# Depthwise convolution by quarters of the channels, in steps between the half blocks of the gated product

## The chip, the cores and the metric

The kernel runs on one core of one Trainium2 chip. The metric is the device time of one execution in microseconds (us), as the median of several runs. Its engines are TensorE (PE, matmuls, with its weight loads PEld), VectorE (DVE), ScalarE (ACT), GpSimd (POOL) and SyncE (SP, whose queue issues the loads of the weights). They work side by side and wait for each other by semaphores. PSUM is the memory that matmuls write to, cut into buffers that are used in turn.

## The reference

A backbone of two layers over 256 context and 256 latent tokens (512 in all, D = 1024): layer 0 mixes tokens with a Conformer convolution, layer 1 with a bidirectional mLSTM, and each is followed by an MLP. The change lies in the convolution of layer 0:

```python
def conformer_conv(u, rows, w_pw1, b_pw1, w_dw, b_dw, ln_g, ln_b, w_pw2, b_pw2):
    a = u @ w_pw1 + b_pw1
    a = a[..., :CONV_DIM] * jax.nn.sigmoid(a[..., CONV_DIM:])
    ...
    a = jax.nn.silu(layer_norm(a + b_dw, ln_g, ln_b))
    return a @ w_pw2 + b_pw2
```

Where the dots are, `a` goes through a depthwise convolution with 31 taps, in rows of 64 tokens for the latent stream and over all 256 for the context. `u` is the input scaled and shifted by the adaLN map (`silu(c) @ ada_w`, 1024 x 6144 per layer), whose later columns give the gates and shifts of the layer's other steps. All is fp32.

## The kernel before, in words

**Products.** A large product takes its weights in column blocks of 128. A tile `raw` of 1 MB (two blocks) is loaded through SP's queue into one of three buffers; each block is split into a rounded part `wh` (ACT, L153) and a rest `wl` (DVE, L154, 128x1024), and every product of 128x128 by 128x512 is three matmuls: `wh` by the input's high part (L176), by its low part (L179), and `wl` by the high part (L180). A block of the gated product (`pw1`) is 8 x 3 = 24 of them.

**The start.** In the start loop, the adaLN map of the first two parts is made and the input split, and four blocks of `pw1` are accumulated beside it. They end with `pw1_epi`: for the gate half a sigmoid on ACT (L740), for the other a product on DVE (L744), which goes back to token order by four transposes (L747) into `A`. Then `gemm` (L215, steps at L218) runs the other 12 blocks, with `pw1_next` behind each.

**The convolution.** It is done as a Fourier transform of 128 points over the tokens. For each of four token tiles, `spectral(h, tt)` takes 512 channels at a time: a forward transform on PE (L762 for the context's tiles 0 and 1, with windows over neighbouring tiles; L767 for the latent tiles 2 and 3, two matmuls over 64 rows each), a multiplication by the spectrum's cosine and sine parts `Hc`, `Hs` on DVE (L776, L777), the inverse transform (L787, four matmuls into two column halves), the bias (L794) and the statistics (L795). It is called from `pw1_epi` for four tiles in a row, once when half of the channels are there and once at the end (`f % 4 == 3`). With the second half, `token_norm(tt)` (L799 on) joins the statistics, takes 1/sqrt by four Newton steps on a column of 128 values (`rsqrt`, L549 on), and applies the norm on DVE (L806).

**Tables.** The transforms' cosines come from a polynomial on DVE over 128x384 and 128x256 elements (L654 to L671), written before the gated product; the windows `ge32`, `lt32`, `ge96` are made on POOL, the spectrum by four matmuls over 31 rows (L693).

**Order.** A scheduler places each instruction on its engine's queue by its own estimate, in the order of the code where that does not decide; `keep_in_program_order` pins an instruction, `tc.issue_after(x)` puts what is inside behind x. Within `gemm`, two units of the adaLN map (`ada_g1`, L317) stand behind the blocks of `Z.fd`. Behind `gemm` come the loads of `pw2`, four units `ada_s2`, the activation `silu(0)` (transposes L845, ACT L848 and L849, DVE L850, the split at L153 and L154), and the product `pw2` with `ko=4`: its first four blocks are accumulated side by side, feature tile by feature tile, as the activation comes. The fifth block begins at 195.53 us of the trace.

## Time and profile before

| what | value |
|---|---|
| runs | 1729.02, 1731.77, 1736.95 us; median 1731.77 |
| the profiled execution | 1730.22 us, of which the span of its instructions 1728.5 us |
| mean granted clock of TensorE | 0.994 |
| gated product and first half of the convolution | 47.0 to 149.5 us of the span |
| second half, norms, activation, first four blocks of `pw2` | 149.5 to 195.5 us |

A page of the profile shows one execution on the slowest core. Busy times are by engine; in the view of windows each row is a stretch, with the busy us and the number of instructions of each engine, then PEclk (the granted clock of TensorE as a share of full speed), the share of DMA engines that were busy, and GB/s. A row of the timeline is start, duration, engine, line, operation, output and inputs, shape and count; in brackets the idle time of the engine ahead of it, and who ended it. Durations of neighbouring matmuls overlap, since they are pipelined: what one costs is the distance to the next start. An fp32 matmul has two records there, an fp32r matmul one.

### The profile page before, as it was taken

How to read it: one execution, taken by the hardware profiler on the slowest of the kernel's cores; microseconds unless marked ns; L12 is line 12 of the kernel's file. 1: busy time of each engine (PE TensorE's matmuls, PEld its weight loads, DVE VectorE, ACT ScalarE, POOL GpSimd, SP SyncE). 2: the span in 40 equal slices, each digit the busy share in tenths (PEclk: the TensorE clock that was granted, in tenths of full speed). 3: DMA queues.
4: the chain of work that ended last, by engine and by line, in shares of the span. 5: the costliest groups of instructions: out<-in, count | busy, mean ns of one | idle time of the engine just before them, and what ended most of it. 6: DMA issues, size and time to landing. Idle time of an engine off the chain costs nothing.

```text
span 1728.5 us, 23701 instructions
## 1 busy us (share of the span) xinstructions
PE 1688.9 (98%) x9270; PEld 1387.1 (80%) x9270; DVE 1064.0 (62%) x1918; ACT 743.1 (43%) x1193; POOL 61.3 (4%) x98
## 2 busy tenths in 40 slices
PE   8999999999999999999999999999999999989997
PEld 5655898878888999986688899888877878758886
DVE  5456895666645776772243663564487786777667
ACT  4311663231324465542232532442467564534453
POOL 0000000000000000000000000000011130030001
PEclk9999999999999999999999999999999999999999
DMA  9323524444423055568675753454445555656552
GB/s 361 144 106 129 191 74 171 152 140 147 146 98 146 26 177 168 161 215 280 239 222 178 248 173 116 153 187 167 169 173 190 194 192 191 243 212 213 184 186 95
DMA packets 69535, 300.58 MB, mean 174 GB/s; under 512 B 7026, under 2 KB 21874, under 8 KB 38704
## 3 DMA queue, kind: packets, MB, share of 16 engines
q1 hardware_dynamic: 51760, 284.39, 47.1%
q10 hardware_dynamic: 17664, 14.69, 2.6%
q8 instruction: 73, 1.20, 0.3%
q14 instruction: 38, 0.31, 0.1%
HBM read 283.32 MB, written 15.73 MB: 173 GB/s over the span
## 4 chain that ended last, share of the span: by engine, by line
PE 92%; DVE 4%; ACT 2%; DMA 1%; issue 1%; POOL 0%; SPq 0%; DVEq 0%; ACTq 0%; POOLq 0%
PE mm L176 17%; PE mm L180 17%; PE mm L179 17%; PE mm L189 7%; PE mm L190 3%; PE mm L206 3%; PE mm L207 3%; PE mm L205 3%; PE cv L207 2%; PE cv L205 2%; PE cv L206 2%; PE fl L317 2%; PE fl L718 1%; PE cv L787 1%; DVE wl L154 1%; PE ln L176 1%
## 5 line engine op out<-in xcount | busy, mean ns | idle before, releaser
L154 DVE TENSOR_TENSOR wl<-raw,wh 128x1024 fp32r<-128x1024 f32 x348 | 427.5, 1232 | 283.9 <-ACT wh L153 281.9
L153 ACT CAST wh<-raw 128x1024 fp32r<-128x1024 f32 x348 | 362.7, 1050 | 533.4 <-PE mm L179 319.8
L179 PE MATMUL mm<-u,wh 128*128 128x256 f32 (+1 forms) x960 | 322.7, 337 | 0.0
L176 PE MATMUL mm<-u,wh 128*128 128x256 f32 (+1 forms) x832 | 273.2, 330 | 6.1 <-DVE E L1003 2.5
L180 PE MATMUL mm<-u,wl 128*128 128x256 f32 (+1 forms) x832 | 272.2, 328 | 0.0
L179 PEld LDWEIGHTS mm<-u,wh 128*128 128x128 f32 x960 | 183.5, 191 | 18.2 <-DVE mv L553 0.8
L176 PEld LDWEIGHTS mm<-u,wh 128*128 128x128 f32 x832 | 159.2, 192 | 26.9 <-ACT wh L153 6.5
L180 PEld LDWEIGHTS mm<-u,wl 128*128 128x128 f32 x832 | 159.6, 192 | 16.0 <-DVE wl L154 1.7
L176 PE MATMUL mm<-xm,wh 128*128 128x512 f32 x256 | 102.9, 402 | 0.0
L205 PE MATMUL mm<-wh,xl 128*128 128x512 f32 x256 | 101.2, 396 | 0.0
L206 PE MATMUL mm<-wh,xl 128*128 128x512 f32 x256 | 100.9, 394 | 0.0
L180 PE MATMUL mm<-xm,wl 128*128 128x512 f32 x256 | 100.3, 392 | 0.0
L207 PE MATMUL mm<-wl,xl 128*128 128x512 f32 x256 | 99.6, 392 | 0.1
L176 PE MATMUL mm<-hid,wh 128*128 128x512 f32 (+1 forms) x256 | 93.3, 365 | 0.0
L179 PE MATMUL mm<-hid,wh 128*128 128x512 f32 (+1 forms) x256 | 92.8, 363 | 0.0
L180 PE MATMUL mm<-hid,wl 128*128 128x512 f32 (+1 forms) x256 | 92.8, 363 | 0.0
L189 PE MATMUL mm<-x,wh 128*128 128x512 f32 x248 | 86.8, 399 | 4.8 <-DVE x L1548 4.3
L393 DVE SCALAR_TENSOR_TENSOR S<-ar,cs,S 128x512 f32<-128x512 f32 x56 | 40.8, 750 | 60.5 <-DMA ar<-ada_w 60.4
L179 PE MATMUL mm<-qq,wh 128*128 128x272 f32 x256 | 73.9, 289 | 0.0
L176 PE MATMUL mm<-qq,wh 128*128 128x272 f32 x256 | 73.5, 288 | 0.0
L180 PE MATMUL mm<-qq,wl 128*128 128x272 f32 x256 | 73.5, 288 | 0.0
L189 PE MATMUL mm<-u,wh 128*128 128x512 f32 x192 | 68.7, 399 | 0.0
(482 smaller groups left out, 3296.5 us busy)
## 6 DMA issues: line engine op xcount, KB each, us to landing
raw<-w SPq DMA_DIRECT2D x64, 1024.0 KB, 4.9
raw<-wo SPq DMA_DIRECT2D x32, 1024.0 KB, 4.9
raw<-ada_w SPq DMA_DIRECT2D x28, 1024.0 KB, 4.9
ar<-ada_w SPq DMA_DIRECT2D x80, 256.0 KB, 3.4
raw<-wv SPq DMA_DIRECT2D x16, 1024.0 KB, 6.2
raw<-wqT SPq DMA_DIRECT2D x16, 1024.0 KB, 5.2
raw<-wq SPq DMA_DIRECT2D x16, 1024.0 KB, 4.9
raw<-wk SPq DMA_DIRECT2D x16, 1024.0 KB, 4.9
```

What stands on the lines that cost most here:

```text
L153: c = nc.scalar.copy(hi, src)
L154: nc.vector.tensor_tensor(lo, src, hi.bitcast(F32), op=ALU.subtract)
L176: a = nc.tensor.matmul(ps, wh, xh, start=start, stop=False)
L179: nc.tensor.matmul(ps, wh, xl, start=False, stop=False)
L180: nc.tensor.matmul(ps, wl, xh, start=False, stop=stop)
L189: todo = [lambda s_, e_: nc.tensor.matmul(ps, wh, r[0], start=s_, stop=e_), lambda s_, e_: nc.tensor.matmul(ps[:, :n], wl, r[0][:, :n], st ...
L190: lambda s_, e_: nc.tensor.matmul(ps[:, :n], wl, r[0][:, :n], start=s_, stop=e_)]
L205: nc.tensor.matmul(ps, xh, wh, start=start, stop=False)
L206: nc.tensor.matmul(ps, xl, wh, start=False, stop=False)
L207: nc.tensor.matmul(ps, xh, wl, start=False, stop=stop)
L317: a = nc.tensor.matmul(ps[32 * j:32 * j + 32], cs[:, kt, 14 - 2 * v:46 - 2 * v], blocks[kt], start=first and kt < 4, stop=last and kt >= 4 ...
L393: nc.vector.scalar_tensor_tensor(a, w, c, a, op0=ALU.mult, op1=ALU.add)
```

## The change

- The convolution goes by four quarters of 256 channels instead of two halves of 512. `spectral` is a generator: its first step is the forward transform with one multiplication on DVE by both parts of the spectrum (`HS`), its second the inverse with bias and statistics.
- Three of the quarters are side jobs of the gated product, at the middle and the end of each of its 12 blocks as `Z.jobs` says; each job does the forward part of one tile and the inverse of the tile before. The last quarter stays behind the product.
- The tables, windows and spectrum are side jobs too, the tables pinned, with the part that the spectrum needs first.
- One `ada_s2` unit moves into the loop (`Z.s2`), the `ada_g1` units move two blocks earlier (`Z.fd`); the load of the gate weights becomes the last side job.
- `token_norm(s)` does two tiles at once, on columns of two values, with three Newton steps of three operations; half of its application goes to ACT. DVE's work on tiles 2 and 3, and its splits of `pw2`'s weights, are put behind the norm of tiles 0 and 1.

```diff
 class Z:
-    fd = [3, 6, 7]
+    fd = [1, 4, 5]
+    s2 = [8]
+    jobs = [1, 1, 0, 1, 0, 1, 1, 1, 1, 1, 1, 1, 1, 1, 1, 1, 0, 1, 1, 1, 1, 1, 0, 0]
...
     def split(hi, lo, src):
         c = nc.scalar.copy(hi, src)
-        nc.vector.tensor_tensor(lo, src, hi.bitcast(F32), op=ALU.subtract)
+        with tc.issue_after(behind[0]) if behind else nullcontext():
+            nc.vector.tensor_tensor(lo, src, hi.bitcast(F32), op=ALU.subtract)
...
-    def gemm_steps(w_ap, groups, rhs, n, epi, ko=0, pre=None):
+    def gemm_steps(w_ap, groups, rhs, n, epi, ko=0, pre=None, mid=None):
...
+                            if mid and kt == 3:
+                                mid(2 * (gi * 2 + m))
                     if kh == kh_n - 1:
                         epi(gi * 2 + m, pss[m])
+                    if mid:
+                        mid(2 * (gi * 2 + m) + 1)
...
-        for _ in range(4):
-            nc.vector.tensor_scalar(q, r, r, v, op0=ALU.mult, op1=ALU.mult)
+        for _ in range(3):
+            nc.vector.tensor_tensor(q, r, r, op=ALU.mult)
+            nc.vector.tensor_tensor(q, q, v, op=ALU.mult)
             nc.vector.scalar_tensor_tensor(r, q, -1.5, r, op0=ALU.add, op1=ALU.mult)
...
-    for t_ in (tab[:, 0:3 * L], tab[:, 3 * L:5 * L]):
+        for t_ in (tab[:, 3 * L:5 * L], tab[:, 0:3 * L]):
...
+            yield
...
+    CH = 256
+    HS = padp.tile([P, 4, 2, CH], F32, name="HS")
+
+    def spectrum():
+        nc.sync.dma_start(bdw, wdw_d[NTAP:NTAP + 1, :].broadcast_to([P, D]))
+        for h_ in range(2):
+            wd = F()[:NTAP, :]
+            nc.sync.dma_start(wd, wdw_d[0:NTAP, h_ * 512:(h_ + 1) * 512])
+            for k, w_ in enumerate((WC, WS)):
+                ps = psum("ln")
+                pinned(nc.tensor.matmul(ps, w_[:NTAP, :], wd, start=True, stop=True))
+                nc.scalar.activation(HS[:, 2 * h_:2 * h_ + 2, k, :], ps.rearrange("p (a c) -> p a c", a=2), AF.Identity, scale=cf)
+            yield
...
-        if f % 4 == 3:
-            for tt in range(4):
-                spectral(f // 4, tt)
...
-            nc.vector.tensor_tensor(p1, xf, Hc[:, sl], op=ALU.mult)
-            nc.vector.tensor_tensor(p2, xf, Hs[:, sl], op=ALU.mult)
+            p_ = F().rearrange("p (k c) -> p k c", k=2)
+            nc.vector.tensor_tensor(p_, xf.rearrange("p (o c) -> p o c", o=1).broadcast_to([P, 2, CH]), HS[:, i], op=ALU.mult)
+            ps_.insert(0, p_)
+        yield
...
-    def token_norm(tt):
+    def token_norm(s):
...
+        for j in range(2):
+            for h, eng in enumerate("VS"):
+                y = Y[2 * s + j][h]
+                if eng == "V":
+                    end = nc.vector.tensor_scalar(y, y, r[:, j:j + 1], q[:, j:j + 1], op0=ALU.mult, op1=ALU.add)
+                else:
+                    nc.scalar.activation(y, y, AF.Identity, scale=r[:, j:j + 1], bias=q[:, j:j + 1])
+        return end.ins
...
+    def side_jobs():
+        yield from tables()
+        yield from windows()
+        yield from spectrum()
+        prev = None
+        for i in range(3):
+            for tt in range(4):
+                g_ = spectral(i, tt)
+                next(g_)
+                if prev:
+                    next(prev)
+                prev = g_
+                yield
+        next(prev)
+        yield from gate_rows()
...
+    def beside(i):
+        for _ in range(Z.jobs[i]):
+            next(jobs, None)
+
+    gemm(pw1, range(6), u, T, pw1_next, mid=beside)
...
+    last = [spectral(3, tt, "mm" if tt % 2 else "cv") for tt in range(4)]
+    ada_s2.mm()
+    for tt in range(2):
+        next(last[tt])
+    ada_s2.mm()
+    for tt in range(2):
+        next(last[tt])
+    normed = token_norm(0)
+    with tc.issue_after(normed):
+        for tt in range(2, 4):
+            next(last[tt])
         ada_s2.mm()
+        for tt in range(2, 4):
+            next(last[tt])
+        token_norm(1)
     ada_s2.end()
...
+    behind.append(normed)
     for _ in gemm2_steps(pw2, range(4), sact, HALVES, pw2_epi, HD, ko=4, pre=pre2):
```

How the order of the instructions moves shows at three places. In the order, `x4` counts matmuls.

First DVE where the gated product begins, before. L744 are the products of the first two feature tiles, L662 to L671 the polynomial of the tables:

```order
L670 SCALAR_TENSOR_TENSOR F_509<-F_509,F_510 128x384
L666 TENSOR_SCALAR tab<-F_523 128x256
L670 SCALAR_TENSOR_TENSOR F_509<-F_509,F_510 128x384
L667 TENSOR_TENSOR F_524<-tab 128x256
L671 SCALAR_TENSOR_TENSOR tab<-F_509,tab 128x384
L668 TENSOR_SCALAR F_523<-F_524 128x256
L744 SCALAR_TENSOR_TENSOR E_585<-mm_114,vecs,E_585 128x512
L670 SCALAR_TENSOR_TENSOR F_523<-F_523,F_524 128x256
L744 SCALAR_TENSOR_TENSOR E_594<-cv_116,vecs,E_594 128x512
```

The same place after (L774 is the product, L157 the weight split, L658 to L667 the one-column constants):

```order
L157 TENSOR_TENSOR wl_588<-raw_521,wh_587 128x1024
L659 SCALAR_TENSOR_TENSOR pc<-pc 128x1
L660 TENSOR_SCALAR pc<-pc 128x1
L661 TENSOR_SCALAR pc<-pc 128x1
L662 TENSOR_SCALAR pc<-pc 128x1
L664 TENSOR_SCALAR pc<-pc 128x1
L665 TENSOR_SCALAR pc<-pc 128x1
L666 TENSOR_TENSOR pc<-pc 128x1
L774 SCALAR_TENSOR_TENSOR E_501<-mm_114,vecs,E_501 128x512
L774 SCALAR_TENSOR_TENSOR E_510<-cv_116,vecs,E_510 128x512
L667 TENSOR_SCALAR pc<-pc 128x1
L668 TENSOR_SCALAR tab<-F_539,pc 128x128
```

The products have moved from within the wide polynomial to ahead of it; all that is left ahead of them is weight splits and one-column operations.

Second PE within a block of the loop, before (`mm` is the block's sum, `u` the input's parts):

```order
L176 MATMUL mm_901<-u_267,wh_905 128x512
L179 MATMUL mm_901<-u_268,wh_905 128x512
L180 MATMUL mm_901<-u_267,wl_906 128x512
L176 MATMUL mm_901<-u_313,wh_905 128x512
L179 MATMUL mm_901<-u_314,wh_905 128x512
L180 MATMUL mm_901<-u_313,wl_906 128x512
```

After, in the middle of a block (L790 the forward transform of tile 0, L815 the inverse of the step before):

```order
L183 MATMUL mm_890<-u_267,wl_895 128x512
L790 MATMUL cv_911<-A,ge_683 128x256
L790 MATMUL cv_911<-A,lt_686 128x256
L790 MATMUL cv_910<-A,tab 128x256
L815 MATMUL ln_919<-F_881,tab 64x256
L815 MATMUL ln_919<-F_879,tab 64x256
L815 MATMUL ln_919<-F_881,tab 64x256
L815 MATMUL ln_919<-F_879,tab 64x256
L179 MATMUL mm_890<-u_313,wh_894 128x512
L182 MATMUL mm_890<-u_314,wh_894 128x512
L183 MATMUL mm_890<-u_313,wl_895 128x512
```

Seven short matmuls stand between two groups of three of the gated product; before, none did in this place.

Third PE in the tail, before: `fl` are the adaLN sums, L845 the transposes of the activation, L787 the last inverse:

```order
L787 MATMUL cv_1212<-F_1209,tab 64x512
L787 MATMUL cv_1212<-F_1205,tab 64x512
L317 MATMUL fl_1290<-raw_1293,cs 32x512 x3
L317 MATMUL fl_1290<-raw_1303,cs 32x512 x4
L317 MATMUL fl_1290<-raw_1305,cs 32x512 x4
L845 MATMUL ln_1357<-ident,u_576 128x128
L845 MATMUL ln_1376<-ident,u_576 128x128
L317 MATMUL fl_1290<-raw_1315,cs 32x512
L787 MATMUL cv_1247<-F_1243,tab 64x512
L787 MATMUL cv_1247<-F_1239,tab 64x512
L787 MATMUL cv_1247<-F_1244,tab 64x512
L787 MATMUL cv_1247<-F_1240,tab 64x512
```

After (L324 the adaLN sums, L922 the transposes):

```order
L795 MATMUL cv_1346<-A,tab 128x256
L795 MATMUL mm_1355<-A,tab 128x256
L795 MATMUL mm_1354<-A,tab 128x256
L324 MATMUL fl_1055<-raw_1300,cs 32x512 x4
L324 MATMUL fl_1055<-raw_1362,cs 32x512 x4
L815 MATMUL ln_1376<-F_1352,tab 64x256
L815 MATMUL ln_1376<-F_1350,tab 64x256
L815 MATMUL ln_1376<-F_1352,tab 64x256
L815 MATMUL ln_1376<-F_1350,tab 64x256
L815 MATMUL ln_1383<-F_1360,tab 64x256
L324 MATMUL fl_1055<-raw_1364,cs 32x512 x4
```

Before, the activation's first transposes stand ahead of the last tile's inverse; after, the inverses of tiles 2 and 3 (`ln_1376`, `ln_1383`) come first, and two adaLN pieces stand between the last forward transforms and them.

## The prediction

> **What bounds the kernel now.** The page first: the span, the engines' busy shares and the chain of work that ended last.

> ```profile
> span 1728.5 us, 23701 instructions
> ...
> PE 1688.9 (98%) x9270; PEld 1387.1 (80%) x9270; DVE 1064.0 (62%) x1918; ACT 743.1 (43%) x1193; POOL 61.3 (4%) x98
> ...
> PE 92%; DVE 4%; ACT 2%; DMA 1%; issue 1%; POOL 0%; SPq 0%; DVEq 0%; ACTq 0%; POOLq 0%
> ```

> The reader is to see that TensorE (PE) is the bound: 98% of 1728.5 us busy, 92% of the chain. Moving work from one place on PE to another therefore gains nothing; only time in which PE waits, runs at a lower clock, or starts a group late can be won. So I read next how much of that the changed stage holds, in the view of windows: the gated product from its first full block to its last (47.0 to 149.5), the tail until the fifth column block of the next product starts (149.5 to 195.5), and the stretch behind it; then shorter stretches around the holes.

> ```profile
> core 0: us, PE busy (x) PEld busy (x) DVE busy (x) ACT busy (x) POOL busy (x), PEclk, DMA share, GB/s
> 47.99:51.40 3.41, 1.22 (x4) 0.59 (x4) 3.41 (x9) 1.97 (x3) 1.28 (x6) 1.00 0.05 14
> 51.41:54.82 3.41, 3.41 (x12) 1.35 (x12) 3.41 (x6) 0.00 (x0) 0.46 (x3) 0.50 0.19 33
> ...
> 58.24:61.64 3.40, 3.39 (x9) 1.03 (x8) 0.00 (x0) 2.07 (x4) 0.00 (x0) 1.00 0.96 388
> 61.65:65.06 3.41, 3.41 (x13) 2.92 (x14) 0.00 (x0) 1.84 (x3) 0.00 (x0) 0.50 0.44 187
> ...
> 170.88:174.29 3.41, 1.68 (x6) 0.48 (x8) 3.41 (x17) 0.00 (x0) 0.00 (x0) 1.00 1.00 416
> 149.50:195.50 46.00, 42.49 (x242) 21.30 (x242) 37.93 (x118) 15.31 (x32) 0.00 (x0) 1.00 0.58 214
> 47.00:149.50 102.50, 99.87 (x421) 65.44 (x423) 48.01 (x80) 25.16 (x33) 1.75 (x8) 0.97 0.31 114
> 195.50:277.00 81.50, 81.21 (x657) 76.02 (x655) 68.13 (x184) 50.90 (x112) 0.00 (x0) 1.00 0.25 90
> ```

> PE stands idle for 102.50 - 99.87 = 2.6 us in the loop and 46.00 - 42.49 = 3.5 us in the tail, and two stretches of 3.41 us ran at half clock (PEclk 0.50), which loses 1.7 us each, 3.4 us together. That is 9.5 us in all, and the whole possible gain apart from group starts. From 195.5 on PE is dense (81.21 of 81.50 us) and its order is the same in both kernels from about 260 us, so what is won or lost at 195.5 arrives at the end unchanged.

> **The holes in the loop.** The timeline of PE, with one row of VectorE (DVE), where the loop begins:

> ```profile
> 48.12 0.50 PE L176 MATMUL mm<-u,wh 128*128 128x512 f32 x1 [0.57 <-ACT wh L153]
> ...
> 50.91 0.47 PE L176 MATMUL mm<-u,wh 128*128 128x512 f32 x1 [2.06 <-DVE E L744]
> ...
> 57.71 3.88 PE L693 MATMUL ln<-F,tab 31*128 31x512 f32 x8
> ```

> ```profile
> 50.02 0.75 DVE L744 SCALAR_TENSOR_TENSOR E<-mm,vecs,E 128x512 f32<-128x512 f32 x1
> ```

> The first gated product L744, which frees the PSUM buffer for the next block, stands behind the polynomial of the tables on DVE and starts only at 50.02; PE waits 0.57 + 2.06 = 2.63 us. In the changed order the two products stand behind two weight splits and eight one-column operations, ahead of all wide table work. I take 0.3 us as what is left: **-2.3 us** (ends -2.6, nothing left, and -1.6, one split of 1.2 us that comes too early).

> The half clock follows right behind a stretch in which PE was busy for only 1.22 of 3.41 us, and right behind one that was full (3.39) but held mostly the eight 31-row matmuls L693; a stretch with 1.68 busy (170.88) brought none. With the wait gone the first cause goes. The second goes because the spectrum's four matmuls now come as two pairs, each between full-height matmuls. **-3.4 us** (ends -3.4 and 0).

> [...]

> **Pairs of 64-row matmuls.** Forward transforms of token tiles 2 and 3 use half the rows each, and two that stand side by side run together:

> ```profile
> 159.41 1.13 PE L767 MATMUL mm<-A,tab 64*128 64x512 f32 x4
> ...
> 162.41 1.12 PE L767 MATMUL mm<-A,tab 64*128 64x512 f32 x2
> ...
> 164.47 1.12 PE L767 MATMUL mm<-A,tab 64*128 64x512 f32 x2
> ```

> Four records (two matmuls) side by side take 1.13 us, two records alone 1.12. Of a 512-column matmul 0.86 us is the stream itself (two records of 0.43, below). Before, each half has one pair together and one apart: 6 groups of 0.86 = 5.16 us. In the order of after, seven of the eight half-wide pairs stand together and one in the tail is apart: 9 groups of 0.43 = 3.87. **-1.3 us**, if half the columns take half the time. The other transforms are the same columns in all (104 matmuls of 256 in place of 52 of 512) and come out even by that rule.

> **More turns.** What an insertion costs the stream of the gated product shows here:

> ```profile
> 100.52 0.39 PE L179 MATMUL mm<-u,wh 128*128 128x512 f32 x1
> 100.84 1.08 PE L787 MATMUL cv<-F,tab 128*64 128x512 f32 x4
> 101.85 0.51 PE L180 MATMUL mm<-u,wl 128*128 128x512 f32 x1
> 102.28 1.08 PE L787 MATMUL cv<-F,tab 128*64 128x512 f32 x4
> 103.29 0.50 PE L176 MATMUL mm<-u,wh 128*128 128x512 f32 x1
> 103.63 0.39 PE L179 MATMUL mm<-u,wh 128*128 128x512 f32 x1
> ```

> ```profile
> 66.64 0.39 PE L176 MATMUL mm<-u,wh 128*128 128x512 f32 x1
> ...
> 72.77 0.39 PE L176 MATMUL mm<-u,wh 128*128 128x512 f32 x1
> ...
> 80.25 0.39 PE L176 MATMUL mm<-u,wh 128*128 128x512 f32 x1
> ...
> 149.12 0.39 PE L180 MATMUL mm<-u,wl 128*128 128x512 f32 x1
> ```

> From 72.77 to 80.25 stand 33 matmuls: 0.227 us each. From 100.52 to 103.63 are 3 of these (0.68) and two insertions of two records deep (0.86 each): 2.40 of 3.11 us, so an insertion costs 0.36 us beside its stream, 0.18 for each change of kind. A second count: from 66.64 to 149.35 the order holds 256 such matmuls (58.0) and 19.5 us of transposes, adaLN and transforms; the time is 82.7, and less 1.3 us of visible waits 3.9 us are left for 29 changes, 0.14 each. I take 0.16. Counted in the two orders, the loop goes from 36 changes to 60 and the tail loses 3: 21 x 0.16 = **+3.4 us** (ends +2.9 and +4.0).

> **New waits in the loop.** An inverse transform now needs the DVE product of the step before, half a block earlier (12 matmuls of 0.227, 2.7 us, between most steps). On DVE a product can stand behind a weight split of 1.2 us and a bias addition, and DVE is busy for 48 of 102.5 us in the loop before; so nearly all are in time. Where a step follows at a block's end, the gated product and its transposes stand in the same queue. I put **+0.7 us** for all twelve (ends 0, and +4 if every step waited a third of a microsecond). The iotas, masks, table operations and the combined multiplication by the spectrum cost PE nothing so long as DVE keeps this slack; the gate weights' load, moved to the end of the side jobs, and the adaLN loads, moved up, share three raw buffers and SP's queue with the gated product's weights, and with a DMA share of 0.31 in the loop I put nothing for them.

> **The tail.** Its holes before are one of 2.79 us and three small ones:

> ```profile
> 172.61 1.04 PE L317 MATMUL fl<-raw,cs 128*32 128x512 f32 x2 [2.79 <-DMA raw<-ada_w]
> ```

> The releaser named is an adaLN load, but behind it the inverse L787 needs products that DVE makes among the Newton chains of three norms, so both were late. After the change, half of the transforms and one adaLN unit have left the tail: work that moved, not gain. In the new order DVE does the norm of tiles 0 and 1 and only then the four products of tiles 2 and 3, and PE's last two inverses wait for these. The chain is 13 dependent small operations; their pace:

> ```profile
> 218.05 0.16 DVE L526 RECIPROCAL lc<-lc 128x2 f32<-128x2 f32 x1
> 218.24 0.16 DVE L527 SCALAR_TENSOR_TENSOR lc<-lc,lc 128x2 f32<-128x2 f32 x1
> 218.43 0.69 DVE L533 TENSOR_TENSOR L<-ident,lc 128x512 f32<-128x512 f32 x1
> ```

> At 0.19 us each that is 2.5 us, with the two wide applications (0.5 each) and the sums ahead 3.8; PE has some 1.4 us of adaLN and forward work beside it, so it waits about 2.4. Then the activations of the first half come at ScalarE's (ACT) pace, as before:

> ```profile
> 176.81 0.56 ACT L848 ACTIVATE S<-ln,vecs 128x256 f32<-128x256 f32 x1 [25.10 <-PE ln L845]
> ...
> 192.25 0.41 ACT L153 CAST u<-S 128x256 fp32r<-128x256 f32 x1
> ```

> Eight steps took 192.25 - 176.81 = 15.4 us there. The two norm applications given to ACT come ahead of these steps, in time in which ACT is idle (15.31 of 46 us busy). Another 0.8 us I put for small waits among the steps: 3.2 in place of 3.5, **-0.3 us** (ends -3.5, no wait left, and +2.8, the wait twice as long, or with a stretch at half clock for 1.7 us).

> **The sum.** -2.3 - 3.4 - 1.3 + 3.4 + 0.7 - 0.3 = -3.2 us. The profiled execution took 1730.22 us, 1.72 beside its span; less 3.2 that is 1727.0. The median of the runs shown, 1731.77, lies 1.55 above the profiled one, so I forecast 1728.6 for the median. Half a per cent, 8.7 us, is about what a measurement of this kernel can tell from no change; the forecast lies inside it.

> **Rivals.**

> *Slower: half a matmul costs more than half (chance 0.15).* The change turns 52 transforms into 104. If a 256-column fp32 matmul carries a fixed cost of its own, each of the 52 added pays it in both its records. Break-even with the gain of 3.2 is 3.2 / 104 = 0.031 us a record. The price of a whole turn, 0.10 a record, would give +10.4 - 3.2 = +7.2, 1739. For it: a lone group shows 0.26 over its stream (1.12 for 0.86). Against it: within a group the records follow at 0.43, and the fp32r matmuls halve well:

> ```profile
> 193.11 0.28 PE L180 MATMUL mm<-u,wl 128*128 128x256 f32 x1
> ...
> 194.55 0.28 PE L180 MATMUL mm<-u,wl 128*128 128x256 f32 x1
> ```

> Twelve in 1.44 us are 0.120 each at 256 columns against 0.227 at 512: 0.007 over half, which for 104 records would be +0.7. [...]

> *Much faster: the holes close altogether (0.13).* No wait in the tail, none added in the loop: -3.2 - 3.2 - 0.7, and 0.5 less for turns, is -7.6, 1724; with luck in the order of the norm 1722. Against it: the 13 operations stand ahead of the products in DVE's own order.

> *The half clock stays (0.14).* Another cause, or the new wait of 2.4 us in the tail, keeps both stretches: -3.2 + 3.4 = +0.2, 1732. For it: in the tail 1.0 us of work in 3.41 would be under the 1.22 that brought it. Against it: 1.68 did not, and the window would have to lie just so. [...]

> *Steps stall PE in the loop (0.08).* If DVE's products come late at each of the 12 steps by one split, 12 x 1.2 = 14 us less the 0.7 counted: +10, 1742. Against it: 48 of 102.5 us busy on DVE.

> **How the numbers follow.** My forecast, -6 to +1 us, has the other 0.50. The range that holds 8 in 10 goes from 1722.5 (the holes closed) to 1737.0 (a third part of a turn's cost for each record more than break-even): it leaves out the most of the stalls, half of the slower rival and a little of the fast one. Faster by over 0.5% needs -8.7 us, nearly all of the 9.5 that there is: 0.11. Slower by as much: the stalls and the upper part of the half-width rival, 0.09. Within: 0.80.

> **What would show it.** In the profile after: no wait over 0.5 us on PE before 60 us, and no PEclk of 0.50 between 48 and 65; transforms of 256 columns at 0.215 us a record, and insertions of three full matmuls and an inverse that cost about 0.36 beside their stream; the end of the gated product about 7 us later than 149.5 and the fifth block of the next product at about 192; one wait of 2 to 3 us in the tail before an inverse, released by DVE. Wrong are: records at 0.25 or more, waits on DVE at many steps, or a time under 1722.5.

## The result and the profile after

The changed kernel takes 1736.03 us (median of 20 runs) against 1731.74 for the kernel before (20 runs): ratio 1.0022, 95% interval 1.0014 to 1.0030. That is some 4 us slower, where 3 us faster was forecast. The time lies inside the stated range (1722.5 to 1737.0), but the interval leaves out both no change and any gain.

The page of the changed kernel, to be laid beside the one before:

```profile
span 1735.1 us, 23906 instructions
...
PE 1693.6 (98%) x9374; PEld 1400.3 (81%) x9374; DVE 1064.9 (61%) x1910; ACT 746.6 (43%) x1197; POOL 60.3 (3%) x98
```

Nothing on it says why. The view of windows does. The rows are laid on the grid of 3.41 us in which this execution's clock changed (the four stretches at half clock begin at 74.77, 173.76, 183.99 and 282.98 us, which are 29, 3 and 29 times 3.41 us apart), each weak stretch with the one behind it; the last two are the loop and the tail.

```profile
core 0: us, PE busy (x) PEld busy (x) DVE busy (x) ACT busy (x) POOL busy (x), PEclk, DMA share, GB/s
...
71.36:74.77 3.41, 2.60 (x9) 1.19 (x7) 0.00 (x0) 0.43 (x1) 1.03 (x5) 1.00 0.43 161
74.77:78.18 3.41, 3.41 (x8) 2.26 (x8) 0.00 (x0) 1.14 (x3) 0.00 (x0) 0.50 0.05 20
...
170.34:173.75 3.41, 1.06 (x8) 0.16 (x8) 3.06 (x14) 1.52 (x2) 0.00 (x0) 1.00 0.88 334
173.76:177.17 3.41, 2.75 (x10) 1.23 (x11) 2.49 (x6) 0.00 (x0) 0.00 (x0) 0.50 0.97 358
180.58:183.99 3.41, 2.00 (x13) 1.47 (x13) 3.38 (x22) 2.99 (x8) 0.00 (x0) 1.00 0.81 308
183.99:187.40 3.41, 3.41 (x18) 3.41 (x18) 2.24 (x10) 2.11 (x6) 0.00 (x0) 0.50 0.03 12
279.57:282.98 3.41, 2.41 (x19) 1.51 (x12) 2.74 (x4) 2.33 (x3) 0.00 (x0) 1.00 0.67 209
282.98:286.39 3.41, 3.41 (x9) 2.62 (x9) 1.68 (x3) 1.93 (x2) 0.00 (x0) 0.50 1.03 418
48.08:159.17 111.09, 110.28 (x538) 74.72 (x537) 61.34 (x123) 24.89 (x33) 1.76 (x8) 0.98 0.36 130
159.17:199.50 40.33, 34.80 (x229) 23.49 (x229) 30.30 (x89) 20.15 (x41) 0.00 (x0) 0.92 0.62 220
```

The reader is to see four stretches at PEclk 0.50 between 70 and 290 us, where the profile before had two. Each follows a stretch in which PE had little to do: the spectrum's pair at 73 (2.60 of 3.41 us busy, 1.56 of it over 31 rows), the tail's wait at 171 (1.06), the first steps of the activation (2.00), and, at 281, the head of a later product (2.41). The holes of the loop itself are nearly gone (111.09 - 110.28 = 0.8 us idle); those of the tail grew to 40.33 - 34.80 = 5.5 us. The waits in the timeline of PE, and the loads in SP's queue that the first of them hangs on:

```profile
73.21 2.21 PE L718 MATMUL ln<-F,tab 31*128 31x512 f32 x4 [0.81 <-DMA F<-wdw_d]
...
172.68 1.06 PE L324 MATMUL fl<-raw,cs 128*32 128x512 f32 x8 [2.36 <-DMA raw<-ada_w]
174.42 2.82 PE L815 MATMUL ln<-F,tab 128*64 128x256 f32 x10 [0.68 <-DVE F L804]
```

```profile
64.43 0.64 SPq L715 DMA_DIRECT2D F<-wdw_d  x2
66.71 15.74 SPq L151 DMA_DIRECT2D raw<-pw  x2
```

The last row holds two issues, at 66.71 and 82.10; the load issued first, the weights of the next two blocks, landed at 77.9 us.

The gated product ends at 159.2 us, where the prediction had some 156.5, and the fifth block of the next product starts at 199.5 us instead of 195.53, where the prediction had about 192. Of these 4.0 us, 1.4 were lost by 47 us already: the matmuls of the start come 0.43 us apart up to 20.2 us in this execution and up to 17.3 in the other, 0.23 apart behind, and half of the 2.9 us between the two is 1.4, an estimate. Behind it the order is the same; of the 2.6 us that the two profiled spans still move apart there, up to 1.7 are the stretch at 283.

### The profile page after: what moved, and what is told of

It is laid out like the page before. It is cut to its first block, busy times and chain, and to the rows that moved or that the text cites. A ratio compares the mean times of both kernels' runs of the same rounds, so it can differ in the third digit from the quotient of the medians.

```text
span 1735.1 us, 23906 instructions
## 1 busy us (share of the span) xinstructions
PE 1693.6 (98%) x9374; PEld 1400.3 (81%) x9374; DVE 1064.9 (61%) x1910; ACT 746.6 (43%) x1197; POOL 60.3 (3%) x98
## 3 DMA queue, kind: packets, MB, share of 16 engines
q8 instruction: 74, 1.21, 0.3%
## 4 chain that ended last, share of the span: by engine, by line
PE 91%; DVE 4%; ACT 2%; DMA 2%; issue 1%; POOL 0%; SPq 0%; DVEq 0%; ACTq 0%; POOLq 0%
PE mm L179 18%; PE mm L182 17%; PE mm L183 17%; PE mm L192 7%; PE mm L193 3%; PE mm L208 3%; PE mm L210 3%; PE mm L209 3%; PE cv L210 2%; PE cv L208 2%; PE cv L209 2%; PE fl L324 1%; DVE wl L157 1%; PE ln L815 1%; PE fl L748 1%; PE ln L179 1%
## 5 line engine op out<-in xcount | busy, mean ns | idle before, releaser
L157 DVE TENSOR_TENSOR wl<-raw,wh 128x1024 fp32r<-128x1024 f32 x348 | 427.8, 1233 | 278.4 <-ACT wh L155 266.7
L179 PE MATMUL mm<-u,wh 128*128 128x256 f32 (+1 forms) x832 | 275.2, 334 | 5.4 <-DVE E L1083 2.5
L179 PEld LDWEIGHTS mm<-u,wh 128*128 128x128 f32 x832 | 159.1, 193 | 32.2 <-issue 8.8
L179 PE MATMUL mm<-xm,wh 128*128 128x512 f32 x256 | 102.8, 402 | 0.0
L179 PE MATMUL mm<-hid,wh 128*128 128x512 f32 (+1 forms) x256 | 93.3, 365 | 0.0
L179 PE MATMUL mm<-qq,wh 128*128 128x272 f32 x256 | 73.5, 289 | 0.0
```

The costliest lines, as they stand in the source:

```text
L157: nc.vector.tensor_tensor(lo, src, hi.bitcast(F32), op=ALU.subtract)
L179: a = nc.tensor.matmul(ps, wh, xh, start=start, stop=False)
```

## The experiments

The theory that I formed on these rows: **the result is a count of stretches at half clock**, about 1.7 us each (half of 3.41, an estimate), each behind a stretch of the 3.41 us grid in which little of the array was used, by rows or by time. The expectations call it the clock theory and, by its second half, the activity theory. The rival: the clock is the same on both sides, and the loss is turns and waits that I priced too low. The runs bear out the theory's second half, the use of the array, as far as 31 rows against 128 go; its first half, the count, they bear out only in part. "Ratio" is always to the kernel before, from runs on the same chip.

**The kernel before once more.** No edit.

> The kernel before once more, to see how much of the clock's behaviour belongs to the program. Clock theory (the result is the count of stretches of 3.41 us at half clock, 1.7 us each): the front (15 to 290 us) has one to three such stretches, at the wait at 48 to 51 us and at the spectrum's 31-row matmuls near 58 to 65 us, but the grid of 3.41 us stretches lies elsewhere, and the span follows the count by 1.7 us each (1727 to 1731). Rival (the clock is the same in every execution; only turns and waits differ): the same two stretches at the same microseconds, and a span within 0.5 us of 1728.5.

```profile
47.02:50.43 3.41, 2.39 (x10) 1.33 (x8) 3.41 (x11) 3.30 (x5) 0.00 (x0) 1.00 0.15 57
50.43:53.84 3.41, 1.70 (x10) 0.46 (x10) 3.41 (x8) 0.66 (x1) 1.75 (x8) 1.00 0.05 14
53.85:57.26 3.41, 2.82 (x12) 2.35 (x13) 3.41 (x6) 0.00 (x0) 0.00 (x0) 1.00 0.62 216
57.26:60.67 3.41, 3.41 (x10) 1.35 (x9) 1.54 (x3) 1.26 (x2) 0.00 (x0) 1.00 1.03 404
60.68:64.09 3.41, 3.40 (x17) 2.17 (x17) 0.00 (x0) 2.58 (x5) 0.00 (x0) 1.00 0.77 300
```

The same program, the same wait (2.08 us, on the gated product), the same eight 31-row matmuls, and no half clock at all between 20 and 300 us. The grid cuts the wait in two here (2.39 and 1.70 us busy), where the first profile had it in one stretch (1.22). The theory said one to three stretches, so its count missed, but the rival's "same stretches in the same places" is refuted. The span is 1727.5, 1.0 less. By the count alone it would be 3.4 less; but the matmul ahead of the wait starts 1.13 us later here (49.25 for 48.12 us), and PE waited 0.67 us more, for a weight split at 54.4. That is most of the difference, not all.

**31 rows or 128, with no idle time.** Six extra matmuls ahead of each of the spectrum's four; their sums are overwritten. The edit shown is that for 31 rows; the other run has `:P` (128 rows) in place of `:NTAP`.

```diff
                 ps = psum("ln")
+                for j in range(6):
+                    pinned(nc.tensor.matmul(ps, w_[:NTAP, :], x[j][:NTAP, :], start=True, stop=True))
```

> The changed kernel with six extra matmuls of 128x512 over 31 rows ahead of each of the four of the spectrum (24 extra, 0.86 us each at full clock, 20.6 us; their sums are overwritten), so that PE is busy without a gap for two runs of 12 us. [...] Rival (only idle time lowers the clock): no half clock in these runs, and 20.6 us over, less the stretch at 75 us: 1754 to 1756.

> The same with the 24 extra matmuls over 128 rows instead of 31 (same columns, same time at full clock). Activity theory: no stretch at half clock inside the two runs of 12 us, 20.6 us over the changed kernel or 1.7 less, span 1753 to 1756, and at least 5 us under the run with 31 rows. Rival (only idle time lowers the clock): the same time as with 31 rows within 2 us.

With 31 rows, windows on this execution's grid:

```profile
73.50:76.91 3.41, 3.41 (x9) 1.48 (x8) 0.00 (x0) 0.00 (x0) 0.00 (x0) 1.00 0.07 27
76.92:80.33 3.41, 3.41 (x5) 1.32 (x4) 1.23 (x1) 1.64 (x2) 0.00 (x0) 0.50 0.01 2
80.33:83.74 3.41, 3.41 (x5) 1.33 (x4) 0.00 (x0) 0.10 (x1) 0.00 (x0) 0.50 0.00 0
```

With 128 rows:

```profile
74.90:78.30 3.40, 3.40 (x9) 1.19 (x7) 0.00 (x0) 0.26 (x1) 0.00 (x0) 1.00 0.05 21
78.30:81.70 3.40, 3.40 (x9) 1.46 (x9) 1.23 (x1) 1.38 (x2) 0.00 (x0) 1.00 0.00 0
81.70:85.10 3.40, 3.40 (x9) 1.17 (x8) 0.00 (x0) 0.03 (x1) 0.00 (x0) 1.00 0.00 0
```

PE is busy for every microsecond of both. With 31 rows the clock falls and stays at half for 20.5 us, and again for 17.1 at the second pair; with 128 rows it never falls there. The spans are 1765.9 and 1749.7 us, 16.2 apart, of which some 13 lie within the two runs of matmuls (72.1 to 91.7 and 98.8 to 117.8 us with 31 rows, 72.3 to 85.0 and 89.4 to 102.2 with 128). The rival is refuted: here the clock fell without idle time. Two sizes were missed. With 31 rows the stretches are six and five, where two or three each were expected, since the runs themselves grew longer at half clock (19.6 and 19.0 us for 12.7 and 12.8). With 128 rows the span is 14.6 us over the changed kernel's, under the 18 to 21 that were expected: the extra matmuls also fill the wait for the taps, and this trace has one stretch at half clock before 300 us in place of four.

**The spectrum over 128 rows.**

```diff
-            wd = F()[:NTAP, :]
-            nc.sync.dma_start(wd, wdw_d[0:NTAP, h_ * 512:(h_ + 1) * 512])
+            wd = F()
+            nc.gpsimd.memset(wd, 0.0)
+            nc.sync.dma_start(wd[:NTAP, :], wdw_d[0:NTAP, h_ * 512:(h_ + 1) * 512])
...
-                pinned(nc.tensor.matmul(ps, w_[:NTAP, :], wd, start=True, stop=True))
+                pinned(nc.tensor.matmul(ps, w_, wd, start=True, stop=True))
```

> The changed kernel with the spectrum's four matmuls over all 128 rows: the weights' tile is cleared on POOL first, so the rows behind the 31 taps add zero. Activity theory: the stretch at half clock at 70 to 85 us, seen in three executions of three with the spectrum in pairs, is gone: 1.0 to 1.7 us faster than the changed kernel, 1734.3 to 1735 (ratio 1.0012 to 1.002). Rival (the wait of 0.81 us for the taps' load lowers the clock there, not the rows): the stretch stays and the time is 1736, or up to 0.5 later for the clearing ahead of the load.

1734.79 us, ratio 1.0013 (1.0003 to 1.0023), within what the theory gave; the interval still touches the changed kernel's 1.0022. In its trace no stretch between 20 and 170 us is at half clock; two in the tail, at 174 and 181, are. The wait for the taps is still there (1.05 us, PEclk 1.00 behind it), so in this trace that wait alone did not lower the clock.

**Matmuls in the tail's wait.**

```diff
             next(last[tt])
+        warm = psum()
+        for k in range(14):
+            tc.keep_in_program_order(nc.tensor.matmul(warm, u[k % DT][0][:, 0:P], u[k % DT][0], start=True, stop=True))
         ada_s2.mm()
```

> The changed kernel with 14 matmuls of 128x512 (0.227 us each, 3.2 us) on PE in the tail's wait for the norm and the adaLN load (2.36 + 0.68 us); their result is not used. Clock theory: the stretch behind the wait is no longer at half clock, which more than pays for the 0.1 to 0.5 us that the filler may overlap: 1 to 1.7 us faster than the changed kernel, 1734.3 to 1735 (ratio to before 1.0012 to 1.002). Rival (turns and waits made the loss): 0 to 0.5 us slower than the changed kernel, 1736 to 1736.5 (ratio 1.0025 or over).

1734.78 us, ratio 1.0011 (0.9997 to 1.0025). The place is as the theory had it, both stretches of the wait at full clock:

```profile
169.70:173.10 3.40, 3.40 (x22) 1.94 (x21) 2.82 (x14) 0.00 (x0) 0.00 (x0) 1.00 0.94 320
173.10:176.50 3.40, 3.40 (x22) 1.84 (x21) 3.29 (x9) 1.52 (x2) 0.00 (x0) 1.00 0.92 364
179.92:183.33 3.41, 1.70 (x13) 1.22 (x13) 2.59 (x14) 2.31 (x6) 0.00 (x0) 1.00 1.00 375
183.33:186.74 3.41, 3.28 (x15) 3.28 (x16) 3.38 (x19) 2.79 (x7) 0.00 (x0) 0.50 0.21 79
```

but the first steps of the activation, 10 us later, fall to half clock all the same, and so does a stretch at 84 us behind the spectrum. The time leans to the theory; by its interval alone it cannot tell.

**Products of tiles 2 and 3 ahead of the norm.**

```diff
+    for tt in range(2, 4):
+        next(last[tt])
     normed = token_norm(0)
-    with tc.issue_after(normed):
-        for tt in range(2, 4):
-            next(last[tt])
-        ada_s2.mm()
-        for tt in range(2, 4):
-            next(last[tt])
-        token_norm(1)
+    for tt in range(2, 4):
+        next(last[tt])
+    ada_s2.mm()
+    with tc.issue_after(normed):
+        token_norm(1)
```

> The changed kernel with the forward transforms and products of tiles 2 and 3 written ahead of the norm of tiles 0 and 1, so that DVE does them in its idle time and PE's last inverses do not wait for the norm. Clock theory: PE's hole in the tail is split in two (before an adaLN load at 172.6, and before the activation's first transposes), each under 2 us; no or one stretch at half clock instead of two: 2 to 3.5 us faster than the changed kernel, 1732.5 to 1734 (ratio 1.0005 to 1.0015). Rival (turns and waits): the norm comes up to 1.2 us later and the activation with it, 0.5 to 1.2 us slower than the changed kernel, 1736.5 to 1737.2 (ratio 1.0025 to 1.003).

1733.22 us, ratio 1.0005 (0.9989 to 1.0020). The wait is not gone, it stands now before the activation's first transposes, as long as before, but the grid's stretches around it held 1.71 and 2.25 us of work and the clock held (PEclk 1.00 in both):

```profile
175.05 0.41 PE L922 MATMUL ln<-ident,u 128*128 128x128 f32 x2 [2.31 <-DVE u L841]
```

The rival had forecast 0.5 to 1.2 us slower (ratio 1.0025 or over), which the interval leaves out; 2.8 us faster was measured. One stretch at half clock is left in this trace, at 75 us behind the spectrum's first pair.

**Both repairs together.** The spectrum over 128 rows, and the products of tiles 2 and 3 ahead of the norm.

> The changed kernel with products of tiles 2 and 3 ahead of the norm and the spectrum over 128 rows. Activity theory: both gains add, 1.0 to 1.7 us below the kernel with the products first alone (1733.2): 1731.5 to 1732.3, ratio to before 1.0000 to 1.0007, and no stretch at half clock between 20 and 300 us in most executions; what is left against the kernel before is turns and the wait of 1.1 to 1.3 us for the gated product at 80 us, which the half clock had hidden. Rival (the half clock only stood in for waits that come back as idle time): 1733 to 1733.5, ratio 1.0007 to 1.0012.

1731.86 us, ratio 0.9998 (0.9986 to 1.0011): the time of the kernel before, as the theory said. So the spectrum and the order of the tail are, together, all of the loss. The clock was not full throughout, though; the trace has a stretch at half clock in the first steps of the activation:

```profile
180.60:184.00 3.40, 3.40 (x19) 3.40 (x18) 2.35 (x7) 3.11 (x6) 0.00 (x0) 0.50 0.52 193
```

**The tables alone, in the kernel before.** The code from `HL = L // 2` to the gate weights stands behind the first two gated products.

```diff
     for m in range(KO0):
         pw1_epi(m, ps0[m])
+    HL = L // 2
+    ij = F()
...
```

> The kernel before with one part of the change alone: the tables' code stands behind the first two gated products, so that these go ahead of the last third of the polynomial on DVE. Clock theory: the wait of 2.06 us shrinks below 1 us and takes the stretch at half clock behind it along, 1.2 + 1.7 = 2.9 us faster than before (ratio about 0.9983); the stretch after the 31-row matmuls stays. Rival (the clock fell for another reason than the wait): only the wait goes, 1.2 us faster (ratio 0.9993), and the stretch at 51 us stays at half clock.

1728.80 us, ratio 0.9982 (0.9969 to 0.9994), as the theory had it (0.9983); the rival's 0.9993 is at the edge. PE still waits 1.21 us for the products at 49.0 and 0.85 us for a weight split at 52.8, 2.06 in all where it was 2.63: only 0.6 us of the 2.8 are idle time won. But the wait is now spread over two stretches, and both stay at full clock; the eight 31-row matmuls still bring theirs:

```profile
48.29:51.70 3.41, 2.70 (x20) 1.69 (x20) 3.41 (x9) 2.91 (x5) 0.19 (x1) 1.00 0.03 7
51.71:55.12 3.41, 2.56 (x14) 1.90 (x11) 3.41 (x5) 0.15 (x1) 3.41 (x1) 1.00 0.58 193
58.53:61.94 3.41, 3.41 (x8) 0.99 (x7) 0.00 (x0) 2.65 (x5) 0.90 (x5) 1.00 0.86 351
61.95:65.36 3.41, 3.41 (x9) 2.52 (x9) 1.22 (x1) 1.13 (x2) 0.00 (x0) 0.50 0.03 12
```

This trace has a second stretch at half clock, in the tail at 171 us. That makes two, as in the first profile before, and the two spans agree (1728.6 and 1728.5). The gain of 2.8 us is one of the medians; that most of it is the clock's is argued, not shown.

**The same with the spectrum over 128 rows**, and then **with matmuls in that tail's wait**: the edits above; the second has ten 128x512 matmuls ahead of the third `ada_s2.mm()`, whose result is not used.

> The kernel before with the tables' code behind the first two products and the spectrum over 128 rows: both repairs of the clock at the start, none of the quarters. Activity theory: the 31-row matmuls' stretch at 62 us goes as well, 1 to 1.7 us faster than with the tables alone (1728.8): 1727 to 1727.8, ratio 0.9972 to 0.9977. Rival (only idle time): 1728.8, ratio 0.998 to 0.9985.

> The kernel before with the tables behind the first products, the spectrum over 128 rows, and ten matmuls of 128x512 (2.3 us) in the tail ahead of the adaLN load for which PE waits 2.8 to 3.3 us; their result is not used. Activity theory: no weak stretch is left between 20 and 300 us, whatever the grid: as fast as the fast half of the runs without the filler (1725.3 to 1726.6), median 1726.5 to 1728, ratio 0.997 to 0.9982. Rival (waits alone): the filler adds 0 to 0.5 us to 1729.0, ratio 0.998 to 0.9985.

1729.02 us, ratio 0.9979 (0.9967 to 0.9990), and 1727.93 us, ratio 0.9973 (0.9961 to 0.9985). The first is undecided: its median lies where the rival put it, its ratio just outside that and just over the theory's. Its twelve runs fall into two groups, 1725.3 to 1726.6 (five) and 1728.4 to 1732.9 (seven), as if one weak place were left, and in its one trace, of a run in the faster group (1726.61), no stretch from 30 to 300 us is at half clock. The second fell within 1725.9 to 1728.4 in all nine runs, as the theory said. Its median is the lowest of the study, and it has none of the quarters.

**The changed kernel once more.** No edit.

> The changed kernel once more. Activity theory: the grid of 3.41 us stretches lies elsewhere against the program, so the stretches at half clock move by up to 3.4 us or one goes or comes, but their places stay the weak ones of this kernel: the spectrum's pairs (70 to 86 us), the wait for the norm (170 to 178) and the first steps of the activation (180 to 188); two to four of them, and a span within 1733 to 1737. Rival (fixed in the program): stretches at the same four places to within 1 us.

```profile
84.09:87.50 3.41, 3.41 (x10) 2.65 (x9) 0.45 (x1) 0.57 (x1) 0.00 (x0) 0.50 0.65 269
172.90:176.30 3.40, 0.96 (x12) 0.27 (x6) 3.23 (x9) 1.52 (x2) 0.00 (x0) 1.00 0.93 325
176.30:179.70 3.40, 3.40 (x18) 0.97 (x14) 1.92 (x5) 0.00 (x0) 0.00 (x0) 0.50 0.96 400
```

```profile
73.39 1.95 PE L718 MATMUL ln<-F,tab 31*128 31x512 f32 x4 [1.33 <-DMA F<-wdw_d]
81.39 0.63 PE L777 MATMUL ln<-ident,E 128*128 128x128 f32 x4 [1.06 <-DVE E L774]
```

Two stretches, the spectrum's second pair at 82 and the wait in the tail, as the theory had it. And where the clock was full between 75 and 78 us, PE came early enough to find a second new wait, 1.06 us for the gated product at 81; the half clock had hidden it in the first profile. That is where the count fails as a price. With two stretches at half clock before 300 us in place of four, the span is 1735.2 us, 0.1 longer than the first, and the fifth block of the next product begins at 200.35, 0.85 later. From 48 to 300 us this execution gains 0.1 us on the first, by the starts of the same instructions. Waits of 1.33 and 1.06 us stand where there were 0.81 and none. So here a stretch at half clock hid a wait of 1.06 us that came when the clock was full, and two stretches fewer won 0.1 us.

**The taps loaded early.** Added to both repairs: the taps and the bias go behind the start loop's loads into a tile of their own.

```diff
+    nc.gpsimd.memset(taps, 0.0)
+    nc.sync.dma_start(taps[:NTAP, :], wdw_d[0:NTAP, :])
+    nc.sync.dma_start(bdw, wdw_d[NTAP:NTAP + 1, :].broadcast_to([P, D]))
...
-            wd = F()
+            wd = taps[:, h_ * 512:(h_ + 1) * 512]
```

> The changed kernel with products first, spectrum over 128 rows, and the taps and the bias loaded behind the start loop's loads into a tile of their own, instead of from the side job. Queue theory: in the changed kernel the taps' loads wait in SP's queue for the tables' buffers and the next weights' load stands behind them (issued at 66.7, landed at 78.4 us), so both PE's wait of 1.0 to 1.4 us for the taps at 73 and that of 1.0 to 1.3 us for the gated product at 80 go: 1.5 to 2.4 us faster than without (1731.9): 1729.5 to 1730.4, ratio to before 0.9985 to 0.9993. Rival (the taps' transfer itself is slow and the wait at 80 is DVE's own order): at most the first wait goes, 0 to 1 us faster, ratio 0.9993 to 1.0000, and a wait over 0.8 us for the gated product at 80 stays.

1730.41 us, ratio 0.9984 (0.9967 to 1.0000), at the fast edge of the queue theory's range by the ratio and at its slow edge by the time; by the intervals alone it can't be told from the kernel without the edit. Both waits, at 73 and at 80 us, are gone from the trace; what stands there now has no idle time ahead:

```profile
72.78 1.88 PE L720 MATMUL ln<-taps,tab 128*128 128x512 f32 x4
78.44 0.63 PE L779 MATMUL ln<-ident,E 128*128 128x128 f32 x4
```

So the taps in the side job held up the weights behind them in SP's queue: in the changed kernel that load, issued at 66.7, landed at 77.9 us, 11.2 us later, where one issued at 47.8 took 4.9. Here it was issued at 69.95, 3.2 us later, and neither wait came. The tail's half clock is still there in this trace:

```profile
172.81:176.20 3.39, 3.08 (x12) 0.78 (x12) 2.30 (x11) 1.25 (x3) 0.00 (x0) 0.50 0.74 295
179.60:183.00 3.40, 3.40 (x17) 3.39 (x17) 2.35 (x6) 2.85 (x6) 0.00 (x0) 0.50 0.28 108
```

## Why the prediction was wrong

**The half clock, -3.4 us: the step that failed.** I took the two stretches of one execution for a property of the program and counted their loss as a gain in full. They are events of a grid that lay elsewhere in each execution seen here (stretches at half clock at 51.41 and 61.65 us in one of the kernel before, none there in the other). In the two traces of the kernel before there are 2 and 0 of them between 20 and 300 us; in the two of the changed kernel 4 and 2. On the mean of these few traces the change adds two where I took two away. Forecast and result are 7.4 us apart (1728.6 and 1736.03): the 3.4 us that were not won and the tail (below) are 5.7 of them, and the rest is about one added stretch of 1.7, an estimate. More than that the count can't bear, as the two traces of the changed kernel show, which agree in span with four and with two. What the runs showed in the term's place is where the loss sits: with the spectrum over 128 rows and the tail in another order, the kernel is back at the time before (ratio 0.9998). I named both sources, the 31-row matmuls and the wait in the tail with its 1.0 us of work, and decided both the wrong way: a pair between full-height matmuls, with the wait of 0.81 us for the taps, was followed by half clock (the stretch at 71.36, PEclk 0.50 from 74.77), and the tail's wait brought the half clock in both traces.

The rival that had this, "the half clock stays", got a chance of 0.14 and a price of +0.2 us, as if no stretch could come in addition.

**The wait at the start, -2.3 us: right.** After the change PE has no wait over 0.25 us between 40 and 73 us, and neither trace of the changed kernel has a stretch at half clock between 48 and 65, as forecast. In the kernel before, moving the tables alone left 2.06 of the 2.63 us and gave 2.8 us by the medians, of which 0.6 are idle time.

**Turns, +3.4 us, and halves, -1.3 us: the prices were right.** An inverse within the gated product costs what I said, and 256 columns cost half of 512:

```profile
151.91 0.39 PE L182 MATMUL mm<-u,wh 128*128 128x512 f32 x1
152.13 0.39 PE L183 MATMUL mm<-u,wl 128*128 128x512 f32 x1
152.45 1.08 PE L815 MATMUL ln<-F,tab 128*64 128x256 f32 x8
153.46 0.50 PE L179 MATMUL mm<-u,wh 128*128 128x512 f32 x1
153.81 0.40 PE L182 MATMUL mm<-u,wh 128*128 128x512 f32 x1
...
163.15 1.03 PE L790 MATMUL mm<-A,ge 128*128 128x256 f32 x4
164.01 0.60 PE L790 MATMUL mm<-A,tab 96*128 96x256 f32 x2
```

From 151.91 to 153.81 are 1.90 us; three matmuls of 0.227 and 0.86 of stream are 1.54, so 0.36 is left, the figure of the prediction. Four records take 164.01 - 163.15 = 0.86 us, 0.215 each, half of 0.43: the slower rival had no ground. The loop as a whole became 111.1 us from 102.7 (46.7 to 149.4): +8.4, of which the clock took 3.4 away and gave 1.7 back, so 10.1 without it; the sum of moved work, turns (24 x 0.16), the lost wait (-2.3) and the new ones (+0.7) was 9.9. The moved work is 7.7 by the records of the two loops: 2.6 of forward transforms, 3.4 of inverses and 1.7 of adaLN.

**New waits in the loop, +0.7 us: the size was near by accident, the place wrong.** No step waited for its products. The waits are for the taps (0.81 and 1.33 us) and, where the clock let PE come early, for the gated product (1.06). The prediction put nothing for the loads that pass each other in SP's queue; it did not list the taps among them. With the taps early, 1.4 us were won by the medians.

**The tail, -0.3 us: wrong by about 2.** The wait for the norm came as worked out (2.4 foreseen; in the second trace 2.44 for DVE and 0.60 for a load, in the first 0.68 for DVE behind 2.36 that are put down to an adaLN load), but the small waits among the activation's steps are 2.5 us of the 5.5, where I put 0.8: 2.0 us more idle time than before, where I had 0.3 less.

**What is left open.** How much of the loss is the clock's and how much is waits is not separated, least of all in the tail: putting the products first moves a wait as well as keeping the clock, and the run with matmuls in the wait was too imprecise for its own effect. With the spectrum repaired on both sides and the taps early, the quarters (1730.41, ratio 0.9984) stand 1.4 to 2.5 us behind the kernel with halves and the tables late (1729.02 and, with the filler, 1727.93; ratios 0.9979 and 0.9973), and the intervals overlap. The prediction's terms without the clock and the tables sum to +2.5.

## What to carry to other kernels

Read a stretch at half clock as an event of one execution (between 20 and 300 us the kernel before had 2 and 0 of them, the changed kernel 4 and 2): profile the same kernel twice before a term rests on it, and price each weak place of a program (little work on PE in 3.4 us, by rows as well as by time) by how often it falls, before and after. Ask too which wait the slow stretch hides; here one of 1.06 us came when the clock was full. Fill short matmuls up to all rows with zeros where the weights' tile allows it: by the medians that gave 1.2 and 1.4 us in the changed kernel (1736.03 to 1734.79, and 1733.22 to 1731.86) and nothing in the kernel before with the tables late (1728.80 to 1729.02). Keep small loads that wait for a buffer out of the queue ahead of large ones: behind the taps a load of weights took 11.2 us instead of 4.9. The interleaving paid 0.14 to 0.18 us for each change of kind on PE here, and could gain only the idle time it filled.

## What the runs showed of the hardware

Busy time alone does not part the stretches shown here. Half clock followed 1.22 of 3.41 us in the kernel before (47.99 us), 1.06, 2.00, 2.41 and 2.60 in the changed kernel, and 1.70 in the run with matmuls in the tail's wait (179.92). It did not follow 1.68 in the kernel before (170.88), 2.39 and 1.70 in the same kernel once more, or 1.71 and 2.25 in the run with the products first. How much of the array must be in use for the clock to stay full was not shown.
